# The first MLP, too, by seven block products, and layer 2's modulation dots moved into the retention

## The chip, the cores and the metric

The kernel runs on one core of a Trainium2 chip. The metric is device time in microseconds, from the first instruction to the last of one execution. TensorE (PE) multiplies, VectorE (DVE) and ScalarE (ACT) do the elementwise work, GpSimd (POOL) issues part of the transfers and does some elementwise work, SyncE (SP) issues the weight transfers.

## The reference

Two independent sequences of 512 tokens and 1024 features go through the same trunk of two layers with their own conditioning vectors. Layer 1 mixes tokens by a four-head retention, layer 2 by grouped-query attention; each layer ends in an MLP that squares a ReLU.

```
for i in range(2):
    sh1, sc1, g1, sh2, sc2, g2 = silu(c) @ mod_w[i] + mod_b[i]     # six chunks of 1024
    h = rmsnorm(x, norm1_g[i]) * (1 + sc1) + sh1
    x = x + g1 * (retention(h) if i == 0 else attention(h))
    h = rmsnorm(x, norm2_g[i]) * (1 + sc2) + sh2
    x = x + g2 * (square(relu(h @ w1[i])) @ w2[i])                 # 1024 -> 4096 -> 1024
return rmsnorm(x, final_g)
```

## The kernel before

All arrays lie with features on the 128 partitions, 512 tokens along the row. Every operand of a matmul is split into a rounded high part and the rest (`split`, L222: a ScalarE copy and a VectorE subtraction), and a product of two 128-blocks is three matmuls (`mm3`, L217). A weight piece is 128 x 1024; SP loads it, ScalarE makes `whi`, VectorE makes `wlo` (L206), up to four pieces ahead.

**Retention.** Eight steps: sequence 0 heads 0 to 3, then sequence 1. A step has 16 weight pieces: four of q and k, four of v, four of the gate g, four of the output. VectorE evicts the scores (L517), takes the statistics of y (L549 and what follows), evicts the gate (L533), the transposed heads (L572, function `tz`), the rope products (L465 to L472) and the output (L586). GpSimd makes the decay strip of the next step (L445 to L455).

**Modulation.** A chunk of a layer's modulation is eight items. An item loads two half tiles of 128 x 512 of `mod_w` by GpSimd (L407) and takes one or two sequences' dot products from them on VectorE (`dot`, L382, a multiply with an accumulator output). Items wait in a list `bg`. `tick` (L159), called for every weight piece, adds `pace[0]` to a counter and, at 1.0, issues the dots of the loaded item behind that piece's `wlo` and the load of the next one. The tiles come from a pool `f2` of eight: four hold the two conditioning rows, two the rope tables while the retention runs. Layer 1's chunks run in the retention at 0.55 items a piece; layer 2's six chunks (48 items, four dots each) run in the first MLP at 1.0.

**MLPs.** The hidden features of an MLP are eight groups of 512. The first MLP takes them plainly: group 0 of each sequence singly, groups 1 to 5 by `Mlp.group`, group 6 and 7 by `ups` and `downs`; group 7 of sequence 1 (four `ups`, four `downs_stream`) is issued between the attention heads of sequence 0 (`weave(a0.heads(), f)`, L1332). The second MLP is `Wide`: two weight blocks and both sequences form a 2 x 2 block product, done by seven products (`seven`, L670) whose operands are sums of blocks; the sums of activations are parked in DRAM and fetched back in split form. It covers groups 1 to 6 and w1 of group 7.

The order in each engine's queue is laid out when the kernel is built, by a scheduler that follows the program and its priorities. Each engine then takes its queue in order.

Of the kernel before, what the change touches and what calls it, by code (L numbers as in the profile page):

```python
# [15 lines left out]
P = 128  # L16
T = 512
KD = 8
EPS = 1e-6
POOL_MLP0 = (2, 4, 6)  # L20
POOL_ATT = (2, 4, 6)
POOL_MLP1 = (5, 7)
ORDER_FIRST = "q0 q1 z0 q2 z1 z2 q3 z3"
ORDER = "g1 g2 g3 q0 z0 q1 z1 q2 z2 z3 q3"
PACE = 0.55
SQ_W = 8
SQ_RAW = 3
SQ_SUM = 4
# [5 lines left out]
def kernel(  # L34
# [45 lines left out]
    line = sm.tile([P, 48], F32, name="line", bufs=1)  # L80
    nc.vector.memset(line, 0.0)
    mixer = ExitStack()
    xfp = mixer.enter_context(tc.tile_pool(name="xfp", bufs=3))
    wp = mixer.enter_context(tc.tile_pool(name="wp", bufs=4))
    rawp = mixer.enter_context(tc.tile_pool(name="rawp", bufs=2))
# [770 lines left out]
    def wide_mlp(wide, m):  # L856
        pairs = [(8 * c + k + 4, 8 * c + k + 8) for c in range(3) for k in range(4)] + [(28, 29), (30, 31)]
        units = [wide.up(f0, f1, n, n < 12) for n, (f0, f1) in enumerate(pairs)]
        first = len(units)
        units += [wide.down(c, 1 + 2 * c, i) for c in range(3) for i in range(4)]  # L860
        wide.forms = [{}, {}, {}]
        late = []
        m.x, m.hh = [[], []], [[], []]

        def fetch_x(i):
            for s, alloc in ((0, ftile), (1, ptile)):
                m.x[s] += [fetch(park[s][2 * i + t], alloc) for t in range(2)]

        def after(n, j):
            for e in late:  # L870
                e[0] -= 1
            if late and late[0][0] <= 0:
                late.pop(0)[1]()
            if n == first - 1 and j == 6:
                fetch_x(0)
            if n == first and j == 5:
                fetch_x(1)
            if first < n < first + 3 and j == 1:
                fetch_x(n - first + 1)
            c, i = divmod(n - first + 1, 4)  # L880
            if i or not 0 <= c < 4:
                return
            if c < 3:
                wide.forms[c][j], cut = wide.fetch_form(lambda k: hhpark[4 * c + k][j - 1], j)
            elif j < 3:
                s = j - 1
                m.hh[s], cut = wide.fetch_form(
                    lambda k: hhpark[12 + k // 2][(0, 3, 1, 2)[2 * (k % 2) + s]], 1)
            else:
                return  # L890
            late.append([3, cut])
# [287 lines left out]
    for step in range(8):  # L1179
# [27 lines left out]
        if step < 7:  # L1207
# [33 lines left out]
        else:  # L1241
# [13 lines left out]
            nm.a()
            d = m.downs(0, 0)
            run(d, 1)
            nm.c()
            nm.m()
            run(d)  # L1260
# [103 lines left out]
    mixer.close()
    sq["f"] = ctx.enter_context(tc.tile_pool(name="sf", bufs=SQ_F, reuse_waits="tile"))
    sq["s"] = ctx.enter_context(tc.tile_pool(name="su", bufs=SQ_SUM, reuse_waits="tile"))
    sq["p"] = ctx.enter_context(tc.tile_pool(name="sq", bufs=1, reuse_waits="tile"))
    nm = Norm(st[1], lambda k: m.x[1][k], modc[1, 4, 1], modc[1, 3, 1], True, keep=hpark[1])
    m.h[1] = nm.h
    wide = Wide(m, hpark, hhpark, lambda i, k: sqtile if i == 6 or (i == 5 and k < 3) else rtile)  # L1370
    wide.negate()
    d = m.downs(0, 0, lambda o: nc.gpsimd.dma_start(park[0][o], m.x[0][o]))
    run(d, 1)
    nm.a()
    run(d, 1)
    nm.c()
    nm.m(4)
    run(d, 1)
    nm.m()
    run(d)  # L1380
    wide.h_fetch(0)
    m.ups(0, 1, [0])
    wide.h_fetch(1)
    m.ups(0, 1, [1])
    wide.h_forms(0)
    m.ups(0, 1, [2])
    wide.h_fetch(2)
    m.ups(0, 1, [3])
    wide.h_forms(1)
    d = m.downs(0, 1, lambda o: nc.gpsimd.dma_start(park[1][o], m.x[1][o]))  # L1390
    run(d, 1)
    wide.h_fetch(3)
    wide.h_forms(2)
    run(d, 1)
    wide.h_forms(3)
    run(d)
    wide_mlp(wide, m)
# [169 lines left out]
```

## Time and profile before

| | |
|---|---|
| time, median of 3 runs | 2608.32 us (2605.57 to 2611.38) |
| profiled execution | 2606.93 us, span 2605.1 us |
| PE busy | 2555.4 us, 98% |
| DVE busy | 1827.3 us, 70% |
| ACT busy | 1017.9 us, 39% |
| POOL busy | 407.5 us, 16% |
| DMA | 359.41 MB, mean 138 GB/s |

The retention lasts until about 920 us, the first MLP until about 1545, the attention until about 1990, the second MLP until the end. A share over the whole span mixes these stages; the rows further down are cut by stage.

### The profile page before, as it was taken

To read this page: it belongs to the slowest core of one execution; us is meant where nothing else is said; L and a number is where in the kernel's file an instruction comes from. 1 tells how busy PE (TensorE), PEld (TensorE's weight loads), DVE (VectorE), ACT (ScalarE), POOL (GpSimd) and SP (SyncE) were. 2 spreads that over 40 slices of the span, in tenths; PEclk is the share of its full clock that TensorE was granted. 3 is DMA by queue.
4 is the path that set the end of the run, shared out by engine and by line. 5 is a ranking of instruction groups with operands and counts; after the bars stand their busy time and mean duration, and the time that the engine had idled before them with its cause. 6 is when DMAs were issued, how large, how long until landed. Compare 5 with 4: busy or idle time off the path is not lost.

```text
span 2605.1 us, 31849 instructions
## 1 busy us (share of the span) xinstructions
PE 2555.4 (98%) x11498; PEld 2098.4 (81%) x11498; DVE 1827.3 (70%) x3432; ACT 1017.9 (39%) x1707; POOL 407.5 (16%) x721
## 2 busy tenths in 40 slices
PE   6999999999999999999999999999999999999998
PEld 4888888888888888888888888878787788878887
DVE  6776577776855776566658566876766776688777
ACT  3333234233233432211221336766754444454422
POOL 2311112212010000000001010100114121142100
PEclk9999999999999999999999999999999999999999
DMA  7544344644433433333334342323347444475423
GB/s 249 190 129 127 128 150 152 215 134 130 134 106 121 131 114 100 98 97 97 97 98 130 125 148 81 109 86 120 98 152 278 154 156 165 145 270 170 140 91 105
DMA packets 114082, 359.41 MB, mean 138 GB/s; under 512 B 17730, under 2 KB 20674, under 8 KB 113924
## 3 DMA queue, kind: packets, MB, share of 16 engines
q1 hardware_dynamic: 57940, 186.61, 22.6%
q0 software_dynamic: 49792, 163.75, 19.0%
q10 hardware_dynamic: 6192, 7.02, 0.8%
q8 instruction: 90, 1.47, 0.2%
q14 instruction: 68, 0.56, 0.1%
HBM read 308.03 MB, written 49.28 MB: 137 GB/s over the span
## 4 chain that ended last, share of the span: by engine, by line
PE 78%; issue 8%; DVE 5%; DMA 4%; POOL 3%; ACT 1%; ACTq 0%; POOLq 0%; DVEq 0%; SPq 0%
PE pm L220 14%; PE pm L219 14%; PE pm L218 14%; PE pa L218 6%; PE pa L219 6%; PE pa L220 6%; PE pa L668 2%; PE pa L666 2%; PE pa L667 2%; PE pm L666 2%; PE pm L668 2%; PE pm L667 2%; POOL hhpark L758 1%; PE pt L1026 1%; DMA f<-in_modw_dram 1%
## 5 line engine op out<-in xcount | busy, mean ns | idle before, releaser
L218 PE MATMUL pm<-r,whi 128*128 128x512 f32 x1696 | 663.4, 393 | 7.9 <-ACT r L1140 5.8
L219 PE MATMUL pm<-r,whi 128*128 128x512 f32 x1696 | 661.4, 390 | 0.1
L220 PE MATMUL pm<-r,wlo 128*128 128x512 f32 x1696 | 660.6, 390 | 0.0
L205 ACT ACTIVATE whi<-raw 128x1024 fp32r<-128x1024 f32 x258 | 272.9, 1059 | 688.7 <-PE pm L219 482.9
L206 DVE TENSOR_TENSOR wlo<-raw,whi 128x1024 fp32r<-128x1024 f32 x258 | 317.9, 1233 | 254.0 <-ACT whi L205 252.1
L218 PEld LDWEIGHTS pm<-r,whi 128*128 128x128 f32 x1696 | 319.1, 188 | 78.1 <-ACT r L1140 6.2
L219 PEld LDWEIGHTS pm<-r,whi 128*128 128x128 f32 x1696 | 319.2, 188 | 67.8 <-DVE r L226 1.4
L220 PEld LDWEIGHTS pm<-r,wlo 128*128 128x128 f32 x1696 | 318.9, 188 | 66.4
L382 DVE SCALAR_TENSOR_TENSOR junk<-f,f 128x512 bf16<-128x512 f32 x344 | 236.5, 688 | 25.5 <-DMA f<-in_modw_dram 20.7
L407 POOL DMA_DIRECT2D f<-in_modw_dram x200 | 108.3, 541 | 925.2 <-DVE junk L382 778.7
L225 ACT ACTIVATE r<-f 128x512 fp32r<-128x512 f32 x177 | 110.2, 631 | 177.9 <-DVE f L607 75.4
L218 PE MATMUL pa<-whi,r 128*128 128x512 f32 x440 | 172.4, 393 | 0.0
L219 PE MATMUL pa<-wlo,r 128*128 128x512 f32 x440 | 172.2, 391 | 0.1
L220 PE MATMUL pa<-whi,r 128*128 128x512 f32 x440 | 171.9, 391 | 0.0
L226 DVE TENSOR_TENSOR r<-f,r 128x512 fp32r<-128x512 f32 x177 | 120.7, 686 | 26.5 <-ACT r L225 26.5
L225 ACT ACTIVATE wh<-rawq 128x512 fp32r<-128x512 f32 x110 | 68.8, 629 | 138.6 <-PE pm L667 82.5
L668 PE MATMUL pa<-r,wh 128*128 128x512 f32 x312 | 121.5, 389 | 0.0
L667 PE MATMUL pa<-r,wh 128*128 128x512 f32 x312 | 121.4, 389 | 0.0
L666 PE MATMUL pa<-r,wh 128*128 128x512 f32 x312 | 121.4, 389 | 0.0
L225 ACT ACTIVATE wh<-sum 128x512 fp32r<-128x512 f32 x104 | 65.0, 629 | 140.9 <-PE pa L667 87.1
L218 PE MATMUL pa<-r,whi 128*128 128x512 f32 x248 | 99.6, 403 | 0.0
L220 PE MATMUL pa<-r,wlo 128*128 128x512 f32 x248 | 99.2, 401 | 0.0
(285 smaller groups left out, 4675.4 us busy)
## 6 DMA issues: line engine op xcount, KB each, us to landing
f<-in_modw_dram POOLq DMA_DIRECT2D x200, 256.0 KB, 3.2
raw<-in_wri_dram SPq DMA_DIRECT2D x92, 512.0 KB, 3.6
raw<-in_w_dram SPq DMA_DIRECT2D x92, 512.0 KB, 3.5
rawq<-in_w_dram SPq DMA_DIRECT2D x72, 512.0 KB, 4.0
r<-hhpark POOLq DMA_DIRECT2D x71, 256.0 KB, 4.3
raw<-in_wro_dram SPq DMA_DIRECT2D x32, 512.0 KB, 3.6
xf<-park POOLq DMA_DIRECT2D x56, 256.0 KB, 3.2
raw<-in_wai_dram SPq DMA_DIRECT2D x24, 512.0 KB, 3.6
```

What stands on the lines that cost most here:

```text
L205: act(hi, raw, AF.Copy)
L206: ins = tt(lo, raw, hi.bitcast(F32), ALU.subtract)
L218: mm(ps, a[0], b[0], start=first, stop=False)
L219: mm(ps, a[0], b[1], start=False, stop=False)
L220: return mm(ps, a[1], b[0], start=False, stop=last)
L225: split.last = act(hi, src_f32, AF.Copy)
L226: split.dve = tt(lo, src_f32, hi.bitcast(F32), ALU.subtract)
L382: stt(junk, w[hf], 0.5, cb[hf], ALU.mult, ALU.mult, accum_out=a[:, 2 * k + hf:2 * k + hf + 1])
L407: nc.gpsimd.dma_start(hv[hf], modw[layer, ch * KD + k][:, hf * T:(hf + 1) * T])
L666: mm(ps, a[0], b[0], start=first and k == 0, stop=False, **more)
L667: mm(ps, a[0], b[1], start=False, stop=False, **more)
L668: mm(ps, a[1], b[0], start=False, stop=k == n - 1, **more)
```

## The change

The wide routine becomes a function `wide_stage` that both layers call: it closes the mixer's pools, opens the routine's own, runs group 0 singly, and then `wide_mlp`. Layer 1's norms now park their results (`keep=`), since the wide routine fetches them; they no longer use GpSimd. After the first MLP the mixer's pools are opened again for the attention. Group 7's w2 of both sequences is done at the end of the first MLP, with the norm of sequence 0 between, so that nothing of the MLP is left for the attention heads. Layer 2's six chunks join the list `bg` at the end of step 2 of the retention, behind layer 1's, and the pace from there on is 1.0. The bounds in steps 3 and 6 (71 and 47) keep the chunks that step 4 and step 7 need in time.

```
 PACE = 0.55
+PACE_LAST = 1.0
...
+    def wide_stage(m, st1):
+        mixer.close()
+        sq["f"] = wide_pools.enter_context(tc.tile_pool(name="sf", bufs=SQ_F, reuse_waits="tile"))
...
+        nm = Norm(st1, lambda k: m.x[1][k], modc[m.L, 4, 1], modc[m.L, 3, 1], True, keep=hparks[m.L][1])
+        wide = Wide(m, hparks[m.L], hhparks[m.L], lambda i, k: sqtile if i == 6 or (i == 5 and k < 3) else rtile)
...
+        wide_mlp(wide, m)
...
         if step == 7:
             nm = Norm(stats_of(fetch(park[0][k]) for k in range(KD)), lambda k: fetch(park[0][k]),
-                      modc[0, 4, 0], modc[0, 3, 0], True)
+                      modc[0, 4, 0], modc[0, 3, 0], True, keep=hparks[0][0])
...
                 for ch in (4, 3, 5):
                     mod_chunk(cb, 0, ch)
-                pace[0] = PACE
+                for ch in (1, 0, 2, 3, 4, 5):
+                    mod_chunk(cb, 1, ch)
+                pace[0] = PACE_LAST
             if step == 3:
-                while len(bg) > 23 or (loaded and len(bg) == 24):
+                while len(bg) > 71 or (loaded and len(bg) == 72):
                     bg_dot()
                     bg_load()
             if step == 6:
-                flush()
+                while len(bg) > 47 or (loaded and len(bg) == 48):
+                    bg_dot()
+                    bg_load()
...
-            m.ups(0, 1, [0, 1, 2, 3])
-            run(m.downs(0, 1))
-    for ch in (1, 0, 2, 3, 4, 5):
-        mod_chunk(cb, 1, ch)
-    pace[0] = 1.0
-    for g in range(1, 6):
-        m.group(g)
-    flush()
-    m.ups(6, 0, [0, 1, 2, 3])
-    run(m.downs(6, 0))
+            flush()
     f2_ctx.__exit__(None, None, None)
+    wide_stage(m, st1)
...
-    m.ups(7, 0, [0, 1, 2, 3])
     run(m.downs(7, 0, parker(0)))
-    nm = Norm(st[0], lambda k: m.x[0][k], modc[1, 1, 0], modc[1, 0, 0], True, POOL_ATT)
-    m.ups(6, 1, [0])
+    nm = Norm(st[0], lambda k: m.x[0][k], modc[1, 1, 0], modc[1, 0, 0], True)
+    d = m.downs(7, 1, parker(1))
...
+    xfp, wp, rawp = mixer_pools(reuse_waits="tile")
...
     def fill():
-        for i in range(4):
-            m.ups(7, 1, [i])
-            yield
-            run(p1, 1)
-        yield from m.downs_stream(7, 1, park[1], st[1])
         yield from p1
...
+    wide_stage(m, st[1])
```

On VectorE, in the first half of retention step 5, before (`wlo<-raw,whi` is the split of a weight piece, `junk` a dot, whose second operand is the half tile it reads, `r<-pa` the split of v):

```order
L206 TENSOR_TENSOR wlo<-raw,whi 128x1024
L382 SCALAR_TENSOR_TENSOR junk,s_3069<-f_5260,f_146 128x512
L382 SCALAR_TENSOR_TENSOR junk,s_3069<-f_5261,f_155 128x512
L382 SCALAR_TENSOR_TENSOR junk,s_3070<-f_5260,f_907 128x512
L382 SCALAR_TENSOR_TENSOR junk,s_3070<-f_5261,f_912 128x512
L206 TENSOR_TENSOR wlo<-raw,whi 128x1024 x2
L382 SCALAR_TENSOR_TENSOR junk,s_3069<-f_5348,f_146 128x512
L382 SCALAR_TENSOR_TENSOR junk,s_3069<-f_5349,f_155 128x512
L382 SCALAR_TENSOR_TENSOR junk,s_3070<-f_5348,f_907 128x512
L226 TENSOR_TENSOR r<-pa,r 128x512 x3
```

The same place in the changed program:

```order
L382 SCALAR_TENSOR_TENSOR junk,s_3093<-f_5327,f_171 128x512
L206 TENSOR_TENSOR wlo<-raw,whi 128x1024
L382 SCALAR_TENSOR_TENSOR junk,s_3094<-f_5326,f_923 128x512
L382 SCALAR_TENSOR_TENSOR junk,s_3094<-f_5327,f_928 128x512
L382 SCALAR_TENSOR_TENSOR junk,s_3093<-f_5428,f_162 128x512
L382 SCALAR_TENSOR_TENSOR junk,s_3093<-f_5429,f_171 128x512
L206 TENSOR_TENSOR wlo<-raw,whi 128x1024
L382 SCALAR_TENSOR_TENSOR junk,s_3094<-f_5428,f_923 128x512
L382 SCALAR_TENSOR_TENSOR junk,s_3094<-f_5429,f_928 128x512
L382 SCALAR_TENSOR_TENSOR junk,s_3093<-f_5470,f_162 128x512
L206 TENSOR_TENSOR wlo<-raw,whi 128x1024
```

Every weight piece now has an item's four dots beside it, and the first dot of an item (5428 behind 5327, 5470 behind 5429) stands directly behind the last dot of the one before.

On TensorE, in the heads of sequence 0 of the attention, before (`ps` are scores, `pt` transposed probabilities, `pa<-r,whi` the first MLP's group 7):

```order
L218 MATMUL ps<-r 128x512
L219 MATMUL ps<-r 128x512
L220 MATMUL ps<-r 128x512
L218 MATMUL pa<-r,whi 128x512
L219 MATMUL pa<-r,whi 128x512
L1026 MATMUL pt<-ident,p 128x128 x2
L220 MATMUL pa<-r,wlo 128x512
L218 MATMUL pa<-r,whi 128x512
```

The same place in the changed program:

```order
L218 MATMUL ps<-r 128x512
L219 MATMUL ps<-r 128x512
L220 MATMUL ps<-r 128x512
L1064 MATMUL pt<-ident,p 128x128 x2
L218 MATMUL ps<-r 128x512
L219 MATMUL ps<-r 128x512
L220 MATMUL ps<-r 128x512
L1064 MATMUL pt<-ident,p 128x128 x2
```

The MLP's matmuls between scores and transposes are gone; no other projection takes their place until the 20th of the 32 score blocks.

## Rows read from the trace of the kernel before

**Rows 1.** Busy time by stretch: us and instructions by engine, clock, DMA.
```profile
1000.00:1500.00 500.00, 500.00 (x2205) 413.35 (x2204) 312.73 (x626) 113.36 (x150) 49.55 (x92) 1.00 0.34 105
2000.00:2500.00 500.00, 490.83 (x2147) 403.01 (x2146) 380.26 (x596) 221.89 (x385) 115.81 (x216) 1.00 0.51 173
1590.00:1660.00 70.00, 69.65 (x335) 56.34 (x334) 56.53 (x135) 50.83 (x130) 0.00 (x0) 1.00 0.22 68
```

**Rows 2.** TensorE in order of time: start, us, instruction.
```profile
480.06 0.39 PE L218 MATMUL pm<-r,whi 128*128 128x512 f32 x1
...
482.78 0.39 PE L218 MATMUL pm<-r,whi 128*128 128x512 f32 x1
...
1580.70 1.03 PE L993 MATMUL pt<-ident,f 128*128 128x128 f32 x8
```

**Rows 3.** VectorE in order of time: first score eviction of steps 4 to 7.
```profile
494.13 1.28 DVE L517 SCALAR_TENSOR_TENSOR f<-pm,dstrip 128x512 f32<-128x512 f32 x2
...
594.33 1.28 DVE L517 SCALAR_TENSOR_TENSOR f<-pm,dstrip 128x512 f32<-128x512 f32 x2
...
697.17 0.68 DVE L517 SCALAR_TENSOR_TENSOR f<-pm,dstrip 128x512 f32<-128x512 f32 x1
...
802.39 1.35 DVE L517 SCALAR_TENSOR_TENSOR f<-pm,dstrip 128x512 f32<-128x512 f32 x2
```

**Rows 4.** Busy time of both halves of step 5, first half of step 7.
```profile
594.33:656.42 62.09, 62.09 (x278) 51.41 (x277) 42.58 (x92) 19.76 (x27) 12.72 (x21) 1.00 0.43 134
656.42:697.17 40.75, 40.75 (x187) 33.82 (x186) 36.66 (x66) 12.25 (x15) 3.95 (x8) 1.00 0.43 137
...
802.39:867.88 65.49, 65.49 (x295) 54.03 (x294) 42.21 (x76) 28.46 (x42) 6.99 (x13) 1.00 0.38 117
```

**Rows 5.** VectorE's busy time in step 5's halves, L382 alone.
```profile
594.33:656.42 62.09, 15.95 (x45) 1.00 0.43 134
656.42:697.17 40.75, 8.40 (x26) 1.00 0.43 137
```

**Rows 6.** VectorE in order of time, step 5; in brackets idle time and its end.
```profile
600.35 0.69 DVE L382 SCALAR_TENSOR_TENSOR junk<-f,f 128x512 bf16<-128x512 f32 x1
...
604.82 0.69 DVE L382 SCALAR_TENSOR_TENSOR junk<-f,f 128x512 bf16<-128x512 f32 x1 [0.94 <-DMA f<-in_modw_dram]
...
614.67 0.69 DVE L382 SCALAR_TENSOR_TENSOR junk<-f,f 128x512 bf16<-128x512 f32 x1
...
615.40 0.69 DVE L382 SCALAR_TENSOR_TENSOR junk<-f,f 128x512 bf16<-128x512 f32 x1
...
616.02 1.88 DVE L226 TENSOR_TENSOR r<-pa,r 128x512 fp32r<-128x512 f32 x3
```

**Rows 7.** GpSimd in order of time, step 5.
```profile
601.35 0.54 POOL L407 DMA_DIRECT2D f<-in_modw_dram  x1 [0.68 <-DVE junk L382]
...
629.36 0.54 POOL L451 DMA_DIRECT2D f<-in_posneg_dram  x1
...
637.47 1.15 POOL L455 TENSOR_TENSOR dstrip<-f 128x448 f32<-128x448 f32 x1
```

**Rows 8.** All loads of line L407, from issue.
```profile
DMA to landing us min/median/max: 2.7/3.3/7.1
```

**Rows 9.** VectorE in order of time, one small operation in steps 5 and 7.
```profile
635.17 1.00 DVE L236 TENSOR_TENSOR s<-s 128x4 f32<-128x4 f32 x1
...
829.19 0.16 DVE L236 TENSOR_TENSOR s<-s 128x4 f32<-128x4 f32 x1
```

**Rows 10.** ScalarE by line from 1590 to 1700: count, busy, mean ns.
```profile
L1009 ACT ACTIVATE p<-ps,s,rq 128x512 f32<-128x512 f32 x25 | 19.4, 775 | 5.4 <-DVE s L1006 5.2
L225 ACT ACTIVATE r<-pt 128x512 fp32r<-128x512 f32 x32 | 18.7, 593 | 6.4 <-PE pt L220 3.4 <-PE pt L993 1.6 <-PE pt L1026 1.2
L1013 ACT ACTIVATE p<-p,s 128x512 f32<-128x512 f32 x18 | 13.0, 722 | 1.6 <-DVE s L1011 1.4
L1009 ACT ACTIVATION_READ_ACCUMULATOR p<-ps,s,rq 128x1 f32 x25 | 4.8, 193 | 0.0
```

More of the change, by code (lines that the diff above doesn't have):

```diff
@@ L19 @@
 EPS = 1e-6
-POOL_MLP0 = (2, 4, 6)
-POOL_ATT = (2, 4, 6)
-POOL_MLP1 = (5, 7)
 ORDER_FIRST = "q0 q1 z0 q2 z1 z2 q3 z3"
@@ L82, with mixer_pools @@
     mixer = ExitStack()
-    xfp = mixer.enter_context(tc.tile_pool(name="xfp", bufs=3))
-    wp = mixer.enter_context(tc.tile_pool(name="wp", bufs=4))
-    rawp = mixer.enter_context(tc.tile_pool(name="rawp", bufs=2))
+    def mixer_pools(**kw):
+        return [mixer.enter_context(tc.tile_pool(name=n, bufs=b, **kw)) for n, b in (("xfp", 3), ("wp", 4), ("rawp", 2))]
+    xfp, wp, rawp = mixer_pools()
     dp = mixer.enter_context(tc.tile_pool(name="dp", bufs=1))
@@ L883, in after @@
             if c < 3:
-                wide.forms[c][j], cut = wide.fetch_form(lambda k: hhpark[4 * c + k][j - 1], j)
+                wide.forms[c][j], cut = wide.fetch_form(lambda k: wide.hhpark[4 * c + k][j - 1], j)
             elif j < 3:
@@ L887, in after @@
                 m.hh[s], cut = wide.fetch_form(
-                    lambda k: hhpark[12 + k // 2][(0, 3, 1, 2)[2 * (k % 2) + s]], 1)
+                    lambda k: wide.hhpark[12 + k // 2][(0, 3, 1, 2)[2 * (k % 2) + s]], 1)
             else:
@@ L895, in wide_mlp @@
             late.pop(0)[1]()
+    wide_pools = ExitStack()
+    def wide_stage(m, st1):
+        mixer.close()
+        sq["f"] = wide_pools.enter_context(tc.tile_pool(name="sf", bufs=SQ_F, reuse_waits="tile"))
+        sq["s"] = wide_pools.enter_context(tc.tile_pool(name="su", bufs=SQ_SUM, reuse_waits="tile"))
+        sq["p"] = wide_pools.enter_context(tc.tile_pool(name="sq", bufs=1, reuse_waits="tile"))
+        nm = Norm(st1, lambda k: m.x[1][k], modc[m.L, 4, 1], modc[m.L, 3, 1], True, keep=hparks[m.L][1])
+        m.h[1] = nm.h
+        wide = Wide(m, hparks[m.L], hhparks[m.L], lambda i, k: sqtile if i == 6 or (i == 5 and k < 3) else rtile)
+        wide.negate()
+        d = m.downs(0, 0, lambda o: nc.gpsimd.dma_start(park[0][o], m.x[0][o]))
+        run(d, 1)
+        nm.a()
+        run(d, 1)
+        nm.c()
+        nm.m(4)
+        run(d, 1)
+        nm.m()
+        run(d)
+        wide.h_fetch(0)
+        m.ups(0, 1, [0])
+        wide.h_fetch(1)
+        m.ups(0, 1, [1])
+        wide.h_forms(0)
+        m.ups(0, 1, [2])
+        wide.h_fetch(2)
+        m.ups(0, 1, [3])
+        wide.h_forms(1)
+        d = m.downs(0, 1, lambda o: nc.gpsimd.dma_start(park[1][o], m.x[1][o]))
+        run(d, 1)
+        wide.h_fetch(3)
+        wide.h_forms(2)
+        run(d, 1)
+        wide.h_forms(3)
+        run(d)
+        wide_mlp(wide, m)
     def attn_tables():
@@ L1076 @@
     psm_ctx.__enter__()
-    hpark = [dram.tile([KD, P, T], F32, name=f"hpark{i}") for i in range(2)]
-    hhpark = [dram.tile([7, P, T], F32, name=f"hhpark{i}") for i in range(14)]
+    hparks = [[dram.tile([KD, P, T], F32, name=f"hpark{L}_{i}") for i in range(2)] for L in range(2)]
+    hhparks = [[dram.tile([7, P, T], F32, name=f"hhpark{L}_{i}") for i in range(14)] for L in range(2)]
     park = [dram.tile([KD, P, T], F32, name=f"park{i}") for i in range(4)]
@@ L1251 @@
                 m.x[0] = [fetch(park[0][k], ftile, nc.scalar) for k in range(KD)]
-            nm = Norm(st1, lambda k: m.x[1][k], modc[0, 4, 1], modc[0, 3, 1], True, POOL_MLP0)
-            m.h[1] = nm.h
             m.ups(0, 0, [3])
[L1255 to L1260, printed above, removed]
-            m.ups(0, 1, [0, 1, 2, 3])
-            run(m.downs(0, 1))
-    for ch in (1, 0, 2, 3, 4, 5):
-        mod_chunk(cb, 1, ch)
-    pace[0] = 1.0
-    for g in range(1, 6):
-        m.group(g)
-    flush()
-    m.ups(6, 0, [0, 1, 2, 3])
-    run(m.downs(6, 0))
+            flush()
     f2_ctx.__exit__(None, None, None)
-    r2p = mixer.enter_context(tc.tile_pool(name="r2p", bufs=8))
+    wide_stage(m, st1)
     st = [Stats(), Stats()]
@@ L1279, in parker @@
         return after
-    m.ups(7, 0, [0, 1, 2, 3])
     run(m.downs(7, 0, parker(0)))
-    nm = Norm(st[0], lambda k: m.x[0][k], modc[1, 1, 0], modc[1, 0, 0], True, POOL_ATT)
-    m.ups(6, 1, [0])
+    nm = Norm(st[0], lambda k: m.x[0][k], modc[1, 1, 0], modc[1, 0, 0], True)
+    d = m.downs(7, 1, parker(1))
+    run(d, 1)
     nm.a()
-    m.ups(6, 1, [1])
+    run(d, 1)
     nm.c()
-    m.ups(6, 1, [2, 3])
+    nm.m(4)
+    run(d, 1)
     nm.m()
-    run(m.downs(6, 1, lambda o: nc.gpsimd.dma_start(park[1][o], m.x[1][o])))
+    run(d)
+    wide_pools.close()
+    sq.clear()
+    xfp, wp, rawp = mixer_pools(reuse_waits="tile")
+    r2p = mixer.enter_context(tc.tile_pool(name="r2p", bufs=8, reuse_waits="tile"))
     psm_ctx.__exit__(None, None, None)
@@ L1343 @@
     run(q1)
-    nm = Norm(st[0], lambda k: fetch(park[2][k]), modc[1, 4, 0], modc[1, 3, 0], True, keep=hpark[0])
+    nm = Norm(st[0], lambda k: fetch(park[2][k]), modc[1, 4, 0], modc[1, 3, 0], True, keep=hparks[1][0])
     m.h[0] = nm.h
@@ L1363 @@
     psm_ctx.__enter__()
[L1364 to L1397, printed above, removed]
+    wide_stage(m, st[1])
     def finish(s, st):
@@ L1461 @@
     run(last_out(*b))
+    wide_pools.close()
     psm_ctx.__exit__(None, None, None)
```

## The prediction

> **What bounds the kernel now.** I read the busy times of stretches first, then single stretches in order of time, then the groups by line. In the plain first MLP (1000 to 1500 us) TensorE is busy for all 500 us and issues 2205 matmuls [rows 1]. Inside such a stretch twelve matmuls of 512 columns take 482.78 - 480.06 = 2.72 us [rows 2], so one costs 0.2267 us and a matmul that is left out there is worth that. VectorE is busy for 313 of these 500 us [rows 1]: it has room there. In the retention TensorE is also busy throughout, but with less margin: a head's step lasts 100.2, 102.8 and 105.2 us in steps 4, 5 and 6 (distances of the first score evictions, L517 [rows 3]). I cut a step where the first transposed head is evicted (L572): the first half of step 5 is 62.1 us with 42.6 us of VectorE work, the second 40.8 us with 36.7 us [rows 4]. Of these the modulation dots (L382) are 16.0 and 8.4 us [rows 5], so all else is 26.6 and 28.3 us.
>
> **Matmuls removed.** A pair of 128-column weight blocks for both sequences is 96 matmuls plainly (2 x 2 x 24) and 84 as seven products of 12. The change does this for 14 w1 pairs and 12 w2 units of layer 0: 26 x 12 = 312 matmuls, 312 x 0.2267 = **-70.7 us**. TensorE is the bound of the stage they leave, and the routine already runs in the last quarter of the program: VectorE does 380 us there in 500 [rows 1], so it keeps up.
>
> **What the routine brings with it.** The same routine from 2000 to 2500 us issues 2147 matmuls where the plain stage issues 2205 [rows 1]: 58 x 0.2267 = 13 us are lost at its entry and where the first forms come back. The first MLP gets a second copy of that entry: **+12**, between 4 (its norm finds its inputs in SBUF) and 16. The stores and loads of the parked forms lie beside the matmuls. Norms with parked results cost ScalarE one more pass a block; ScalarE has room in both places.
>
> **The dots moved into the retention.** 48 items (six chunks of eight), each of four dots, leave the first MLP, where they cost nothing, and go to steps 3 to 7, now one item for each weight piece instead of 0.55. Steps 4, 5 and 6 then have 64, 64 and 66 dots; before they had 36, 35 and 12. A dot followed by another dot takes 615.40 - 614.67 = 0.73 us, one followed by something else 616.02 - 615.40 = 0.62 [rows 6], on the mix 0.66. The new order puts 44 of 64 dots in the first half: 26.6 + 44 x 0.66 = 55.6 us of work in a half of 62.1; the second half: 28.3 + 20 x 0.62 = 40.7 in 40.8. Work alone would just fit. What does not fit is the buffers. Of the eight f2 tiles four hold the two conditioning rows and two the rope tables, so one item (two tiles) is in flight: its successor is loaded only after its third dot. In the trace a dot starts at 600.35, GpSimd issues the freed tile's load at 601.35, and the next dot, which idles for it, starts at 604.82 [rows 6, 7]: from the end of the one dot (0.61 later) to the next it is 3.9 us. Landing alone is 3.3 in the median, 2.7 to 7.1 [rows 8]. VectorE takes its queue in order, so where the order has only a weight split (1.14) between two items it stands still, and the weight splits, score evictions and group evictions behind it stand too. Following step 5's rows between the third dot of an item and the first of the next (3.9 less the work between), the ten changes of item in the first half wait 0.2, 3.2, 3.2, 1.5, 2.1, 1.4, 1.0, 3.2, 1.5 and 1.6: 18.9 us. First half 74.5, second 41 us; a step 115 instead of 100.2, 102.8, 105.2: +14.8 + 12.2 + 9.8 = 37 us. GpSimd also makes the decay strip in each of these steps, from 629.36 to 638.6 [rows 7], in the same queue as the loads; an item's own turn of four dots and 3.9 us is shorter, so the load behind the strip is some 2.5 late: 3 x 2.5 = 7.5. In step 7 the rope tables are dead, two items fit and no ring wait is left, but its first half gets 50 dots: 42.2 + 50 x 0.66 = 75.2 in 65.5 [rows 4], +9.7, and its 16 park fetches share GpSimd's queue, +2.8. Step 3 has room. Sum **+57**. Bounds: +10 if every ring wait falls into time in which VectorE would have waited anyhow (then only step 7 grows); +90 if the turn is 5 us (33 changes x 1.1 more).
>
> The Trainium skill, "DMA: Bandwidth & Descriptors", section "Anatomy of one DMA", gives 2.0 us plus bytes over 436 GB/s, so an estimate of 2.6 for these 256 KB. By it the turn would be 0.7 shorter and the whole sum about 20 us smaller, 2608: no change. The trace has 3.3 in the median over 200 such loads [rows 8], so I stay with the row; the case lies at the forecast's low end.
>
> While the strip's arithmetic runs on GpSimd, small VectorE operations stretch: L236 takes 1.00 us at 635.17 and 0.16 at 829.19 [rows 9]. The Trainium skill, "SBUF — State Buffer", section "Who interferes with whom", says that a VectorE instruction with two SBUF inputs contends with a GpSimd instruction that reads SBUF. Every dot is of that kind; by it up to the strip's six operations, the longest 1.15 us [rows 7], so 6.9 at most, could be added to each of three steps: up to 21 us more. The trace has no dot inside a strip, so it is not in my sum.
>
> **Attention loses its filler.** Before, the last group's w1 and w2 for sequence 1 (192 matmuls) lie between the heads of sequence 0, and TensorE is busy 69.65 of 70 us there [rows 1]. They are now done before the attention; the new order has no projection matmul among the first 19 of 32 score blocks. In that stretch TensorE has 57 score and 36 value matmuls and 68 transposes (eight take 1.03 us, so 0.13 each [rows 2]): 21.1 + 8.8 = 30 us. ScalarE has, by head, 4 x (0.775 + 0.193) + 3 x 0.722 = 6.0 for the softmax and 5 x 0.593 = 3.0 behind it [rows 10]: 4.75 x 6.0 + 3 x 3.0 = 37.6, and the order puts some 20 more operations of about half a microsecond there (squares, splits, the norm), so 48. So 18 us are open by work alone, and the softmax passes five times between engines: **+23**, from 5 (if half hides under later matmuls) to 35.
>
> **Sum.** -70.7 + 12 + 57 + 23 = +21.3 on the profiled execution's 2606.9 (1.4 below the median of the runs): **2628**. What cannot be told from no change is 0.2%, here 2603 to 2614.
>
> **Rivals.**
> *The ring waits vanish* (0.24). The order was laid out for a VectorE that is often idle, and the 62.1 us half leaves 6.5 us over its work. For it: the dots of steps 4 and 5 of before, half as dense, cost TensorE nothing. Against: 18.9 is three times 6.5, and instructions are taken in order. Then retention +10, attention +18 (nothing lost to the passes), entry +12: -31, **2576**. The change wins as soon as retention costs under 70.7 - 12 - 23 = 36 us.
> *GpSimd's queue decides* (0.15). Loads stand behind the strip's input and, in step 7, behind fetches that wait for a free buffer. For it: the strip holds that queue for 9 us a step [rows 7] and the slowest landing is 7.1 [rows 8]. With a turn of 5 us the retention is at +90: **2661**. Against: the median landing.
> *The saving is not reached* (0.06): the first MLP's stage, with the routine's sums on VectorE, stalls for 30 us and not for 12: **2646**. Against: VectorE has less to do there, as the dots are gone.
>
> **Chances.** The forecast has 0.55; its own range, from a turn of 3.4 to 4.3 and attention from 12 to 30, is 2606 to 2652. For 8 in 10 the range takes in most of the first rival and of the second: 2580 to 2664. Faster than 2603: the first rival and a little of the forecast's low end, 0.26; within 0.2%: the rest of that end, 0.10; slower 0.64.
>
> **What would show it.** Right: in steps 4 to 6 the distance of first L517 rows grows to about 115 us; dots wait for modulation loads 15 us and more in each; TensorE waits on VectorE there, with its busy share near 90%; the step's first half takes nearly all of it. Step 7's first half is about 78. The stretch from the first gated output (L617) to the attention is some 60 us shorter at over 215 matmuls in 50 us. The first half of sequence 0's heads shows TensorE idle for some 20 us, with ScalarE or VectorE as releaser. Wrong: steps still at 103 us (the ring is hidden), or heads without idle time.

## The result, and the profile after

The changed kernel takes 2666.65 us (median of 4 runs, 2661.65 to 2674.20) against 2606.95 us of the kernel before, measured beside it: a ratio of 1.023, 95% interval 1.0201 to 1.0259. It is slower by some 60 us where the forecast had 21, and 2.6 us outside the range.

The page's first lines and its row of the clock, for the changed kernel:

```profile
span 2664.4 us, 32643 instructions
PE 2528.7 (95%) x11186; PEld 2056.7 (77%) x11186; DVE 1991.8 (75%) x3800; ACT 1120.2 (42%) x1949; POOL 526.2 (20%) x947
...
PEclk9999999999998999999999999899999999999999
```

TensorE is busy for only 27 us less than before, although 312 matmuls of 0.2267 us are gone. Where that went is seen by stage. First the busy times from one first score eviction (L517) to the next, so one row is one step (its length, then us and instructions of TensorE, its weight loads, VectorE, ScalarE and GpSimd, the granted clock, the DMA share and GB/s); the last row ends at the first gated output (L617). Before, steps 2, 3 and 7:

```profile
273.45:378.67 105.22, 105.22 (x473) 87.20 (x472) 65.96 (x118) 32.26 (x42) 15.64 (x26) 1.00 0.40 129
378.67:494.13 115.46, 114.78 (x516) 94.52 (x515) 87.67 (x165) 42.64 (x59) 33.61 (x57) 1.00 0.57 184
...
802.39:916.37 113.98, 113.98 (x516) 94.09 (x515) 76.72 (x128) 49.05 (x71) 8.27 (x14) 1.00 0.40 127
```

After, steps 2 to 7:

```profile
273.15:383.13 109.98, 108.22 (x485) 89.33 (x484) 68.97 (x129) 32.29 (x42) 18.86 (x32) 1.00 0.44 136
383.13:506.81 123.68, 110.89 (x480) 88.63 (x479) 99.38 (x210) 42.53 (x59) 37.46 (x63) 0.97 0.55 179
506.81:628.57 121.76, 112.05 (x472) 89.94 (x471) 98.07 (x223) 31.66 (x42) 26.73 (x46) 0.95 0.50 158
628.57:751.63 123.06, 109.79 (x472) 88.73 (x472) 97.54 (x221) 31.71 (x43) 25.32 (x43) 0.96 0.46 145
751.63:877.51 125.88, 109.83 (x462) 88.14 (x463) 96.14 (x221) 31.25 (x42) 26.21 (x45) 0.95 0.45 144
877.51:1002.79 125.28, 116.99 (x511) 93.82 (x510) 104.41 (x245) 52.78 (x80) 24.20 (x45) 0.97 0.58 186
```

Against 105.2 and 115.5 us for steps 2 and 3, 100.2, 102.8 and 105.2 for steps 4 to 6 [rows 3] and 114.0 for step 7, the steps grew by 4.8, 8.2, 21.6, 20.2, 20.7 and 11.3 us. The first L617 stands at 1002.79 instead of 916.37: the retention lost 86.4 us. From there to the first score reduction of sequence 1's attention (1806.76 before, 1864.44 after) 28.7 us are won back, and behind it 1.6 are lost: +59.3 in all, the difference of the spans. That reduction before, and then after:

```profile
1806.76 0.68 DVE L1005 TENSOR_REDUCE s<-ps 128x1 f32<-128x512 f32 x1
```

```profile
1864.44 0.68 DVE L1043 TENSOR_REDUCE s<-ps 128x1 f32<-128x512 f32 x1
```

In steps 4 to 6 VectorE has hardly any time in which it neither works nor waits for a load. Its waits from 506.81 to 877.51, longest first (total us, times, longest):

```profile
DVE junk L382 <- DMA f<-in_modw_dram: 70.4, 46, 4.5
DVE f L533 <- ACT f L532: 3.2, 3, 2.1
DVE wlo L206 <- ACT whi L205: 2.1, 6, 0.8
```

Its work in these three rows is 291.8 us; with the 70.4 us in which it stands for a modulation load that is 362.2 of 370.7 us. TensorE's idle time and its slower clock (0.95 and 0.96 in these rows; 1.00 in the same steps before) go with these waits: e2 below takes the waits away, and both are all but gone with them. Two turns of the buffer, on VectorE and then on GpSimd:

```profile
520.46 0.69 DVE L382 SCALAR_TENSOR_TENSOR junk<-f,f 128x512 bf16<-128x512 f32 x1
...
521.20 0.70 DVE L382 SCALAR_TENSOR_TENSOR junk<-f,f 128x512 bf16<-128x512 f32 x1
...
525.67 0.69 DVE L382 SCALAR_TENSOR_TENSOR junk<-f,f 128x512 bf16<-128x512 f32 x1 [3.78 <-DMA f<-in_modw_dram]
...
533.29 0.69 DVE L382 SCALAR_TENSOR_TENSOR junk<-f,f 128x512 bf16<-128x512 f32 x1 [2.57 <-DMA f<-in_modw_dram]
...
534.87 0.69 DVE L382 SCALAR_TENSOR_TENSOR junk<-f,f 128x512 bf16<-128x512 f32 x1 [0.88 <-DMA f<-in_modw_dram]
```

```profile
521.46 0.54 POOL L407 DMA_DIRECT2D f<-in_modw_dram  x1 [4.59 <-DVE junk L382]
522.25 0.54 POOL L407 DMA_DIRECT2D f<-in_modw_dram  x1 [0.26 <-issue]
...
529.88 0.54 POOL L407 DMA_DIRECT2D f<-in_modw_dram  x1 [0.20 <-issue]
```

The third dot of an item ends at 521.15, the load of the freed tile is issued at 521.46, and the next item's first dot starts at 525.67: a turn of 4.5 us, with one dot of work inside it. That is a long one. Over the 25 items of steps 4 to 6 whose first dot waited more than 0.2 us, the turn is 3.2 to 6.1 us, in the median 4.0; the forecast had 3.9. The next item shows a second wait: its other half tile is loaded only after the fourth dot (529.88), and the first dot that reads it (534.87) stands still again. Of the 70.4 us, 53.3 are waits of first dots and 17.0 are waits for the second half tile.

Behind the retention, the entry of the first MLP, its middle, its end and the heads of sequence 0:

```profile
1050.00:1100.00 50.00, 46.56 (x196) 37.37 (x195) 37.59 (x60) 21.08 (x36) 7.59 (x14) 0.97 0.41 137
1100.00:1150.00 50.00, 50.00 (x222) 41.40 (x221) 34.19 (x53) 21.57 (x37) 13.36 (x25) 1.00 0.56 189
1620.00:1660.00 40.00, 36.80 (x150) 29.76 (x151) 25.12 (x55) 17.98 (x38) 1.08 (x2) 0.91 0.43 133
1696.60:1800.00 103.40, 91.26 (x424) 69.19 (x424) 83.31 (x216) 81.10 (x193) 4.31 (x8) 0.93 0.15 46
```

The routine runs at 222 matmuls in 50 us between its entry and its end. In the heads TensorE is idle for 12.1 of 103.4 us, and at a mean clock of 0.93.

### The profile page after: what moved, and what is told of

Its sections match the earlier page's. It is cut to its first block, busy times and chain, and to the rows that moved or that the text cites. A ratio compares the mean times of both kernels' runs of the same rounds, so it can differ in the third digit from the quotient of the medians.

```text
span 2664.4 us, 32643 instructions
## 1 busy us (share of the span) xinstructions
PE 2528.7 (95%) x11186; PEld 2056.7 (77%) x11186; DVE 1991.8 (75%) x3800; ACT 1120.2 (42%) x1949; POOL 526.2 (20%) x947
## 3 DMA queue, kind: packets, MB, share of 16 engines
q1 hardware_dynamic: 59284, 180.32, 21.6%
## 5 line engine op out<-in xcount | busy, mean ns | idle before, releaser
L218 PE MATMUL pm<-r,whi 128*128 128x512 f32 x768 | 306.7, 402 | 29.8 <-DVE f L572 14.6
L205 ACT ACTIVATE whi<-raw 128x1024 fp32r<-128x1024 f32 x174 | 183.6, 1057 | 339.1 <-DMA raw<-in_wri_dram 106.4
L220 PE MATMUL pm<-r,wlo 128*128 128x512 f32 x768 | 304.6, 397 | 9.1 <-DVE wlo L206 9.1
L219 PE MATMUL pm<-r,whi 128*128 128x512 f32 x768 | 305.6, 398 | 5.5 <-DVE r L313 5.4
L382 DVE SCALAR_TENSOR_TENSOR junk<-f,f 128x512 bf16<-128x512 f32 x344 | 239.6, 696 | 94.1 <-DMA f<-in_modw_dram 91.0
L206 DVE TENSOR_TENSOR wlo<-raw,whi 128x1024 fp32r<-128x1024 f32 x174 | 216.9, 1247 | 89.6 <-ACT whi L205 89.0
L225 ACT ACTIVATE wh<-rawq 128x512 fp32r<-128x512 f32 x228 | 142.5, 629 | 286.6 <-PE pm L667 159.7
L666 PE MATMUL pa<-r,wh 128*128 128x512 f32 x624 | 242.7, 389 | 0.0
L667 PE MATMUL pa<-r,wh 128*128 128x512 f32 x624 | 242.7, 389 | 0.0
L668 PE MATMUL pa<-r,wh 128*128 128x512 f32 x624 | 242.7, 389 | 0.0
L407 POOL DMA_DIRECT2D f<-in_modw_dram x200 | 108.2, 541 | 596.6 <-DVE junk L382 495.8
L218 PEld LDWEIGHTS pm<-r,whi 128*128 128x128 f32 x768 | 147.3, 192 | 65.0 <-issue 15.9
L666 PE MATMUL pm<-r,wh 128*128 128x512 f32 x468 | 182.6, 390 | 1.9 <-ACT wh L225 1.9
L668 PE MATMUL pm<-r,wh 128*128 128x512 f32 x468 | 182.1, 389 | 0.0
L667 PE MATMUL pm<-r,wh 128*128 128x512 f32 x468 | 182.1, 389 | 0.0
L220 PEld LDWEIGHTS pm<-r,wlo 128*128 128x128 f32 x768 | 147.7, 192 | 42.2 <-DVE wlo L206 11.2
L219 PEld LDWEIGHTS pm<-r,whi 128*128 128x128 f32 x768 | 147.9, 193 | 39.8 <-DVE r L313 8.7
L226 DVE TENSOR_TENSOR wh<-sum,wh 128x512 fp32r<-128x512 f32 x208 | 141.4, 685 | 44.1 <-ACT wh L225 42.7
```

The costliest lines, as they stand in the source:

```text
L205: act(hi, raw, AF.Copy)
L206: ins = tt(lo, raw, hi.bitcast(F32), ALU.subtract)
L218: mm(ps, a[0], b[0], start=first, stop=False)
L219: mm(ps, a[0], b[1], start=False, stop=False)
L220: return mm(ps, a[1], b[0], start=False, stop=last)
L225: split.last = act(hi, src_f32, AF.Copy)
```

## The experiments

Ratios are to the kernel before, measured beside each. Three theories stood against each other. RING: VectorE waits in order for the one item that two free tiles allow. WORK: the dots' own VectorE time fills the steps. QUEUE: GpSimd's queue makes the loads late. A fourth, CLOCK, came from the rows above: TensorE's slow stretches cost on their own.

**e1, the order of an item's dots.**

```diff
-            for s in seqs:
-                dot(accs[s], hv, cb[s], k)
+            for hf in range(2):
+                for s in seqs:
+                    dot(accs[s], hv, cb[s], k, (hf,))
```

> The four dots of an item in another order: first both sequences on the first half, then both on the second. A half tile is then free after the item's second dot instead of its third, with the same loads, tiles and VectorE work. RING (steps 4 to 6 are set by VectorE standing still for modulation loads, 70.5 us of waits there and 17.7 from 330 to 506.8 us): each waited change of item gains the length of one dot, 0.7 us, some 35 times in the program: 2642, between 2635 and 2652. WORK (the dots' own VectorE time fills the steps, the waits only fill what is left): 2667. QUEUE (the loads are late because GpSimd's queue is held by the decay strip and the fetches): only the changes behind a strip gain, 2660 to 2667.

Measured: 2643.43 us, ratio 1.0131 (1.011 to 1.0153): 23 us faster than the change as it was. Steps 4 to 6 took 118.6, 116.7 and 117.3 us. VectorE's waits in them:

```profile
DVE junk L382 <- DMA f<-in_modw_dram: 44.5, 37, 3.1
```

Same work, same loads, same queue; only the moment at which a tile comes free moved by one dot. RING holds (2635 to 2652 were expected by it), and WORK and QUEUE as the cause of the whole are out: neither expected more than 7 us.

**e2, two items in flight.**

```diff
-                    mod_chunk(cb, 0, ch)
+                    mod_chunk(cb, 0, ch, alt=ch != 4)
                 for ch in (1, 0, 2, 3, 4, 5):
-                    mod_chunk(cb, 1, ch)
+                    mod_chunk(cb, 1, ch, alt=ch < 4)
```

> Every second item of the chunks that are loaded in steps 4 to 6 goes into the three tiles of the fetch pool, which nothing uses in these steps: two items in flight instead of one, same dots, same number of loads from the same queue. RING: the 70.5 us of waits for modulation loads in steps 4 to 6 nearly vanish, a step falls from 121.8, 123.1, 125.9 us to what VectorE's 98 us of work and TensorE's 105 us leave, 106 to 110: about 2622, between 2608 and 2635. WORK: steps stay above 118 us, 2650 to 2667. QUEUE: each load still waits its turn on GpSimd behind strip and fetches; 7 to 10 us gained at most, 2657.

Measured: 2609.13 us, ratio 1.001 (0.9995 to 1.0025). This edit alone gives 57.5 of the 60 us back, the near end of what RING expected (2608 to 2635). Its steps 4 to 7:

```profile
506.06:613.18 107.12, 107.02 (x474) 88.18 (x474) 100.46 (x235) 32.11 (x42) 30.07 (x47) 0.99 0.59 188
613.18:716.47 103.29, 103.29 (x465) 85.56 (x464) 96.07 (x223) 31.95 (x42) 25.58 (x42) 1.00 0.56 172
716.47:821.35 104.88, 104.88 (x472) 86.94 (x471) 96.07 (x221) 32.08 (x42) 25.22 (x44) 1.00 0.57 174
821.35:945.85 124.50, 117.80 (x508) 95.33 (x507) 100.99 (x234) 51.24 (x78) 23.06 (x43) 0.96 0.55 177
```

With as many VectorE instructions in steps 5 and 6 (223 and 221, against 221 and 221 above) TensorE is busy for all of both steps at a clock of 1.00, and they last 103.3 and 104.9 us, as without layer 2's dots. So in these two steps 96 us of VectorE work in 104 cost nothing, and the loss was the wait alone. Steps 4 and 7 are another matter: no dot waits for a load there, and yet they last 6.9 and 10.5 us longer than before. They have 70 and 49 dots, 51 and 43 of them in the first half. So dots that crowd one half cost time even without a load wait, as the forecast had it for step 7 by VectorE's work; e7, which has 46 and none in these halves, has 103.6 and 114.4 us there.

**e3, the change without layer 2's dots.**

```diff
-                for ch in (1, 0, 2, 3, 4, 5):
-                    mod_chunk(cb, 1, ch)
-                pace[0] = PACE_LAST
+                for ch in range(6):
+                    for s in range(2):
+                        new_col(1, ch, s)
+                        nc.vector.memset(modc[1, ch, s], 0.25)
+                pace[0] = PACE
```

> Leaves out layer 2's modulation: its 48 items are neither loaded nor multiplied, the twelve columns are set to 0.25; layer 0's items go back to 0.55 item a weight piece. What is left of the change is the wide first MLP and the attention without its filler. If the loss is all in the retention (first gated output of the MLP 86.4 us later than before) the retention is again as before: 2666.6 - 86.4 = 2580. If the stages behind it carry part of the loss (loads of the parked forms, the reopened pools, the heads) more than the 28 us that they gain by the two traces: 2600 or more. If the missing GpSimd and DMA traffic also helps elsewhere: under 2575.

Measured: 2582.79 us, ratio 0.9906 (0.9887 to 0.9925). The first L617 stands at 917.89, 1.5 us later than before. So the wide first MLP and the attention without filler gain 24 us together, and nearly all of the retention's 86.4 us comes with layer 2's dots and their loads.

**e4, the filler back between the heads.**

```diff
+    for o in range(KD):
+        nc.gpsimd.dma_start(park[1][o], m.x[1][o])
     run(m.downs(7, 0, parker(0)))
...
     def fill():
+        d = m.downs_stream(7, 1, park[1], st[1])
+        for _ in range(4):
+            run(d, 1)
+            yield
+            run(p1, 1)
+        run(d)
         yield from p1
```

> The last w2 group of sequence 1 (96 matmuls, 21.8 us of TensorE) goes back between the heads of sequence 0, on x tiles fetched again from HBM. In that stretch (1696.6 to 1800 us) TensorE was idle 12.1 us, and it ran 13.7 us at half its clock, which costs 6.8. HEADS WITHOUT FILLER (these 19 us are lost because nothing else is in TensorE's queue): 12 to 18 us gained, about 2652. HEADS BOUND ELSEWHERE (ScalarE and VectorE set the heads' pace, or the refetched tiles wait): the 96 matmuls fill idle time but the heads last longer, 2662 to 2670.

Measured: 2655.85 us, ratio 1.0181 (1.016 to 1.0202): 10.8 us gained, a little under the expected 12 to 18. The heads, from their first reduction to 1800 us:

```profile
1679.40:1800.00 120.60, 116.04 (x564) 91.70 (x563) 103.47 (x252) 94.08 (x213) 12.96 (x24) 0.99 0.30 92
```

Idle time fell from 12.1 to 4.6 us and the clock rose to 0.99: half of the 192 matmuls that the heads had lost were enough for most of it.

**e5 and e9, matmuls of no use ahead of TensorE's waits.** In e5 ten and twenty at two places of a step; e9 has sixteen at the second place:

```diff
             w = piece(wri[n, f])
+            if self.s == 1 and n > 0 and f == 1:
+                spare = abank()
+                for _ in range(16):
+                    mm(spare, self.h[0][0][:, 0:P], self.h[1][0], start=True, stop=True)
             ps = mbank()
```

> The changed kernel with matmuls of no use in front of the two waits that were longest in steps 4 to 6: ten ahead of the first query/key projection of a step, twenty ahead of the second, so TensorE computes something while it waits for VectorE there (0 to 4.8 and 4.6 to 5.0 us a step in the trace), 90 matmuls of 0.2267 = 20.4 us in all. RING (VectorE's queue of work and load waits sets the step, TensorE's waits and its slow stretches are a consequence): the waits shrink, the granted clock may no longer fall behind them, and the time stays, 2660 to 2672. CLOCK (TensorE at half its clock for 51 us in the retention costs 26 us on top): the slow stretches behind these waits vanish and 10 to 20 us are gained, 2647 to 2657.

Measured: 2676.10 us, ratio 1.0264 (1.0249 to 1.028): slower than RING allowed, and nothing gained as CLOCK wanted.

> As the run with matmuls of no use, at one place only: sixteen (3.6 us) ahead of the second query/key projection in steps 4, 5 and 6, where TensorE waited 5.0, 4.6 and 5.0 us for the first transposed head's eviction and its clock stood at half afterwards. The earlier run added 30 a step at two places and was 9.5 us slower; its steps 5 and 6 alone, 246.7 us, were 2.2 shorter. RING: the sixteen fit into the wait and nothing is gained or lost, 2664 to 2671. CLOCK: the slow stretch behind the wait goes, at 6.8 us of half clock 3.4 us a step, 10 us gained, 2657.

Measured: 2660.45 us, ratio 1.0208 (1.0193 to 1.0224), between the two expectations, and not to be told from the change itself (1.0201 to 1.0259). The edit did not do what it was meant to: TensorE's mean clock from 500 to 1000 us is 0.95 in e9, 0.97 in e5 and 0.96 without them, and its waits moved to the transposes ahead (from VectorE's L470, 12.6 us where the place itself had 14.6). Whether the slow clock costs something by itself is therefore not settled by these two; that it does not cost the 26 us is only suggested by VectorE's full rows, and no run took the clock alone away.

**e8, the loads of step 3 taken away, their dots kept.**

```diff
+        held = layer == 0 and (ch == 4 or (ch == 2 and 1 in seqs))
+
         def load(k):
+            if held and fixed:
+                return fixed[0]
             get = xtile if alt and k % 2 else f2tile
             hv = [get(), get()]
+            if held:
+                fixed.append(hv)
```

> The changed kernel, but the sixteen items whose dots lie from the end of step 2 to the end of step 3 (sequence 1's gate and layer 0's second shift) are all multiplied with the first item's tiles: the other fifteen are not loaded, so their weights are left out, and the number of dots and their place stay. Steps 2 and 3 took 110.0 and 123.7 us against 105.2 and 115.5, where the prediction had no loss. RING (VectorE stands 17.7 us there for loads, which delays the norm of sequence 1 and the end of step 3): both steps return to before within 3 us, 13 gained, 2654. WORK (some 28 more dots of 0.66 us in front of the norm's short operations are enough): step 3 stays near 122, 2662 to 2667.

Measured: 2648.93 us, ratio 1.0159 (1.0141 to 1.0178). Step 2 is back at 105.2 us, and the first transposed head of step 3 at 446.09 (before 446.82, changed kernel 456.69): there the loss was the load wait. But step 3's second part took 55.7 us against 47.3 before (50.1 in the changed kernel), so step 3 as a whole stayed at 124.1. The expectation held for one part and failed for the other. That the total came near RING's 2654 is no evidence for step 3: of the 17.7 us gained only 4.4 lie in steps 2 and 3. What delays the end of step 3 stays open: VectorE stands 6.1 us for loads there, in the changed kernel 5.6, and before the change it already stood 5.8.

**e6, e1, e2 and e4 together.**

> The three edits together: two items in flight in steps 4 to 6, dots ordered by half tile, and the last w2 group of sequence 1 between the heads of sequence 0. With two items in flight the order of the dots can help only in steps 2 and 3, where one item is still in flight (17.7 us of load waits), so a few us; the filler gave 10.8 us and lies in another stage. 2609.1 - 10.8 - 4 = 2594 if the gains add, between 2588 and 2600. If the filler's gain depends on the late retention (it does not by RING): 2605 or more.

Measured: 2597.85 us, ratio 0.9971 (0.996 to 0.9982). The gains add, within the expected 2588 to 2600; the 11.3 us below e2 are little more than the filler's 10.8, so the order of the dots gave next to nothing here.

**e7, all dots spread over steps 1 to 7.**

```diff
-                mod_chunk(cb, 0, 1, (1,))
-                mod_chunk(cb, 0, 0, (1,))
-                pace[0] = PACE
+                for ch in (1, 0, 2):
+                    mod_chunk(cb, 0, ch, (1,), alt=True)
+                for L, ch, alt in ((0, 4, 1), (0, 3, 1), (0, 5, 0), (1, 1, 1), ...):
+                    mod_chunk(cb, L, ch, alt=alt)
+                pace[0] = 1.25
             if step == 2:
+                leave(80)
+                pace[0] = 0.4
             if step == 3:
+                leave(72)
+                pace[0] = 1.0
```

(`leave(n)`, a new function, works the list `bg` down to n items at once, loads and dots.)

> As the run with the three edits, and all dots spread over steps 1 to 7: sequence 1's three chunks and layer 0's other three start after step 0 at 1.25 items a weight piece, 0.4 in step 3 (which has the norm), 1.0 in steps 4 to 6, and only 12 dots are left to step 7; every chunk but the one of step 3 alternates between the two pools. Without layer 2's dots the retention reached the MLP at 917.9 us, with two items in flight at 945.9: of these 28 us 11 lie in steps 2 and 3, 8 in step 4's start, 9 in step 7. RING (a dot costs nothing where no load is waited for and VectorE keeps some us over its work): about 20 of the 28 go, 2574, between 2566 and 2584. WORK (each dot costs some of its time wherever it stands, since TensorE and VectorE wait for each other): the 28 us move to steps 1 and 2, 2590 to 2596.

Measured: 2579.18 us, ratio 0.9903 (0.9889 to 0.9917). Steps 1 and 2 took 104.4 and 105.3 us, though they now hold 42 and 60 dots instead of 18 and 16: WORK is out there too. From step 2 on one load wait is left, in step 3's end, on GpSimd and VectorE:

```profile
481.31 0.54 POOL L412 DMA_DIRECT2D f<-in_modw_dram  x1 [0.61 <-DVE mc L394]
...
484.15 0.54 POOL L252 DMA_DIRECT2D p<-in_xs_dram  x1 [1.56 <-DMA park<-p]
484.68 0.54 POOL L412 DMA_DIRECT2D f<-in_modw_dram  x1
```

```profile
488.99 0.69 DVE L387 SCALAR_TENSOR_TENSOR junk<-f,f 128x512 bf16<-128x512 f32 x1 [4.95 <-DMA f<-in_modw_dram]
```

The load at 484.68 does stand behind a reload of sequence 1's x, which waits until the store of sequence 0's has landed. But it is not the one that the dot waited for. It brings the item's other half tile, and nobody waits for it. The dot's tile is loaded from 481.31, hardly held up in GpSimd's queue; the load took 7.7 us to land, at 488.96, and the dot starts at 488.99. The view of the loads issued from 481 to 482:

```profile
DMA to landing us min/median/max: 7.7/7.7/7.7
```

So the reading on which the next expectation rests ("issued at 484.68 behind such a wait") is wrong.

**e10, e7 with the pace at zero in that stretch.**

```diff
                 leave(72)
-                pace[0] = 1.0
+                pace[0] = 0.0
...
                 r = r1
+                pace[0] = 1.0
```

> As the run with all dots spread, but no modulation load is issued while step 3's output projection runs; some 16 dots move to step 7 for it. In that stretch GpSimd's queue also holds the stores of sequence 0 and the reloads of sequence 1, each of which waits for its store to land; in the spread kernel the second load of an item was issued at 484.68 behind such a wait, a dot stood 4.95 us for it until 488.99, TensorE stood 3.8 us behind the dot and its clock was at half for 6.8 us. QUEUE (at this one place GpSimd's order makes the load late): the wait, and the slow stretch behind it, go, 3 to 7 us gained less 1 for step 7: 2575, between 2571 and 2578. RING (the item's own turn makes it late, whatever else is in the queue) or the 16 dots in step 7 cost as much: 2578 to 2583.

Measured: 2573.24 us, ratio 0.9875 (0.9859 to 0.9892): 6 us gained, and the fastest of all, inside what QUEUE expected. Its steps 2 to 5:

```profile
273.15:378.51 105.36, 105.36 (x474) 87.33 (x473) 96.33 (x215) 32.40 (x42) 25.12 (x41) 1.00 0.55 168
378.51:489.43 110.92, 109.59 (x493) 90.30 (x492) 89.51 (x173) 42.14 (x59) 32.01 (x52) 1.00 0.57 180
489.43:593.02 103.59, 103.59 (x466) 85.87 (x465) 93.30 (x205) 32.13 (x42) 23.63 (x41) 1.00 0.54 173
593.02:698.66 105.64, 105.64 (x476) 87.56 (x475) 98.30 (x219) 32.11 (x42) 24.16 (x42) 1.00 0.53 168
```

Step 3 is at 110.9 us and no step from 2 to 7 has a clock under 1.00. But this does not show that QUEUE was right. The edit did not free the stretch of loads: `leave(72)`, which stayed, still issues there. From the first transposed head to the end of step 3 there are 7 modulation loads and 13 dots, where e7 had 10 and 19. And VectorE still stands 4.9 us for loads, now in two waits:

```profile
477.64 0.69 DVE L387 SCALAR_TENSOR_TENSOR junk<-f,f 128x512 bf16<-128x512 f32 x1 [2.41 <-DMA f<-in_modw_dram]
...
485.99 0.69 DVE L387 SCALAR_TENSOR_TENSOR junk<-f,f 128x512 bf16<-128x512 f32 x1 [2.45 <-DMA f<-in_modw_dram]
```

TensorE's wait behind them fell from 3.8 to 1.3 us. Whether the 6 us come from fewer dots, fewer loads or from the one long wait being split is not shown.

## Why the prediction was wrong

The direction and the mechanism came out as forecast; the sizes of two terms did not. **The step that failed is "The dots moved into the retention", +57: it measured 86.4.** By its own parts:

- *"Step 3 has room."* It had not: steps 2 and 3 lost 13.0 us where the sum had nothing. The room was counted in VectorE's share of the step. But already there one item is in flight, and dots that wait for a load stand ahead of operations for which TensorE waits at once: the output's evictions in step 2 (L586, 1.8 us) and sequence 1's norm in step 3 (L273, 4.7 us); before, TensorE had no such wait there. With the loads away (e8) step 2 and step 3's front are as before, 10.2 of the 13.0 us. The other 2.8 lie in step 3's end, and their cause stays open.
- *Steps 4 to 6, +37 for the ring and +7.5 for the strip.* 117.5 us a step were forecast; 121.8, 123.1 and 125.9 came: +62.5 instead of +44.5. The pieces, as means of the three: VectorE's work 97.3 instead of 96.3; waits for loads 23.5 instead of 18.9 + 2.5; and 2.8 us of small gaps, forecast as none. The turn was read almost right (4.0 in the median, not 3.9), and first dots waited 17.8 us a step, a little less than the 18.9 of the sum. What the sum left out is the second half tile of an item, 5.7 us a step. The row that the forecast read its turn from [rows 6, 7] shows just such a wait: the load at 601.35 follows the fourth dot of an item, and the dot at 604.82 is the first to read that second half tile. The strip, for its part, held a load back by 2.3 to 2.9 us in each step, but the dots behind it waited only 1.0 to 1.2. e1 and e2 show that the waits carried the loss: with one dot less in the turn 18 us went from these steps, and with a second item in flight 55.4 of the 62.5.
- *Step 7, +12.5.* It grew by 11.3, and its first half took 79.0 us where 78 was named as the sign.

So the forecast's second bound, a turn of 5 us and +90, was nearer to the truth than its middle, but by luck: the turn was hardly longer than forecast, and the strip in GpSimd's queue cost about 1 us of waiting a step.

The other terms, *matmuls and entry* (-70.7 + 12) and *attention* (+23), come to -35.7 together and measured -28.7. That they come so near is in part chance. The 192 matmuls that moved from the heads into the first MLP are an estimated 43.5 us at 0.2267 each. With these, the first MLP (from the first L617 to the first score reduction, 695.7 us before, 693.9 after) gained 45.4 us and not 58.7: its entry and end cost 25 where +12 was forecast. The attention (from there to sequence 1's first reduction, 194.7 and 167.8) lost 16.7 and not 23. In the heads the loss is 12.1 us idle, and 7 us by the clock (0.07 of 103.4). Missing from the sum was the end of the first MLP: from 1620 to 1660 TensorE issues 150 matmuls, some 26 fewer than fit, at a clock of 0.91; there the mixer's pools are opened again, and TensorE waits 4.2 us for a weight split (L205). The clock was not in the sum at all. After a wait TensorE can issue at half its pace for a few us, so a wait there costs more than its length:

```profile
586.58 0.76 PE L218 MATMUL pm<-r,whi 128*128 128x512 f32 x1 [5.00 <-DVE f L572]
587.14 0.63 PE L219 MATMUL pm<-r,whi 128*128 128x512 f32 x1
587.57 0.63 PE L220 MATMUL pm<-r,wlo 128*128 128x512 f32 x1
587.99 0.63 PE L218 MATMUL pm<-r,whi 128*128 128x512 f32 x1
```

The pitch is 0.43 us instead of 0.2267, and the granted clock is 0.50 from 586.58 to 590.98: the lower of its two levels, 1.2 GHz. In steps 4 to 6 VectorE's full rows suggest that this added nothing, since VectorE set the pace; in the heads it adds to the idle time.

*The rivals.* "The ring waits vanish" was worth 2576. e2 shows what it lacked in steps 5 and 6: not a VectorE with spare time, but a second item in flight. That alone gave 2609; 2573 came only in e10, with the filler back and the dots spread as well. The Trainium skill's formula ("DMA: Bandwidth & Descriptors", "Anatomy of one DMA"), an estimate of 2.6 us for such a load, would have made the turn shorter; the loads land in 3.4 us in the median of the changed kernel, so the row was the better guide.

## What to carry to other kernels

Work that is moved to an engine "with room" needs its inputs there in time: count the buffers that are really free in that stretch, and for each of them the whole turn from the last reader's end to the next reader's start, before counting busy time. An engine that takes its queue in order turns each late load into a delay of everything behind it, also of the short operations for which the matrix engine waits. Here a second item in flight, in three tiles that lay unused, was worth 57.5 us, more than another order of the dots (23) or an even spread (19 on top); and after that the spread dots filled VectorE to nine tenths of a step at no cost.

## What the runs showed of the hardware

Dots beside the decay strip stretch. In step 4, while GpSimd's strip operations run from 567.52 to 574.16:

```profile
567.80 0.89 DVE L382 SCALAR_TENSOR_TENSOR junk<-f,f 128x512 bf16<-128x512 f32 x1
...
568.74 1.00 DVE L382 SCALAR_TENSOR_TENSOR junk<-f,f 128x512 bf16<-128x512 f32 x1
...
569.79 1.51 DVE L382 SCALAR_TENSOR_TENSOR junk<-f,f 128x512 bf16<-128x512 f32 x1
...
572.83 2.42 DVE L206 TENSOR_TENSOR wlo<-raw,whi 128x1024 fp32r<-128x1024 f32 x1 [0.26 <-ACT whi L205]
```

Against 0.69 and 1.22 elsewhere, that is 0.2 + 0.3 + 0.8 + 1.2 = 2.5 us in this step. This is the rule that the forecast cited and left out of its sum (the Trainium skill, "SBUF — State Buffer", "Who interferes with whom"); the trace agrees with it, at about a third of the 6.9 us a step that the strip's length had given as the most. It matters which of the two starts first: the three dots of the changed kernel that began before a strip operation kept their 0.68 us, and of the ten that began inside one, eight took 0.89 to 1.51. In step 6, where a strip operation runs from 817.05 to 817.78:

```profile
816.59 0.68 DVE L382 SCALAR_TENSOR_TENSOR junk<-f,f 128x512 bf16<-128x512 f32 x1
...
817.31 1.00 DVE L382 SCALAR_TENSOR_TENSOR junk<-f,f 128x512 bf16<-128x512 f32 x1
```

The forecast's "the trace has no dot inside a strip" overlooked two such dots in step 3 of the kernel before, at 437.48 and 439.13; both began first, and both took 0.68 us.
